# A decoder trunk on one core: the order of the first feed-forward block's first loads, products and transposes

## The chip, the core and the metric

The kernel runs on one core of a Trainium2 chip. The metric is the device time of one execution in microseconds (us); lower is better. A profiled execution also gives a trace: for every instruction its engine, its start and its duration, what its engine had been waiting for, and for every transfer its issue and its landing. The engines are named as in the trace: PE is TensorE (matmuls; PEld is its weight load), DVE is VectorE, ACT is ScalarE, POOL is GpSimd and SP is SyncE. An engine takes the instructions of its queue in order.

## What is computed

The reference is a trunk of two layers on 512 tokens of 1024 features, all in f32. Each layer runs a half-step gated feed-forward block, a token mixer, a cross-attention and another feed-forward block, with a layer norm after each:

```python
def swiglu_ffn(x, w_in, w_out):
    h = x @ w_in
    g, u = jnp.split(h, 2, axis=-1)
    return (jax.nn.silu(g) * u) @ w_out
...
for i in range(DEPTH):
    m, j = i % N_MIXERS, i // N_MIXERS
    x = layer_norm(a * x + 0.5 * swiglu_ffn(x, ffn_w_in[i, 0], ffn_w_out[i, 0]),
                   ln_g[i, 0], ln_b[i, 0])
    ...
    x = layer_norm(a * x + h, ln_g[i, 1], ln_b[i, 1])
    x = layer_norm(a * x + memory_cross_attention(x, mem, xa_wq[i], xa_wkv[i], xa_wo[i]),
                   ln_g[i, 2], ln_b[i, 2])
    x = layer_norm(a * x + 0.5 * swiglu_ffn(x, ffn_w_in[i, 1], ffn_w_out[i, 1]),
                   ln_g[i, 3], ln_b[i, 3])
return x
```

The change lies in the very first `swiglu_ffn`, in its first matrix product `x @ w_in` (1024 x 5632).

## The kernel before

**Numbers.** TensorE multiplies in a reduced format, so each f32 operand is split in two parts: ScalarE casts it (`hi`, line 120) and VectorE subtracts the cast from the original (`lo`, line 121). A product is three matmuls per block: high weights with high tokens, high weights with low tokens, low weights with high tokens (lines 205 to 207; the very first product has its own loop, line 681, with all 16 matmuls of the high weights first and then the 8 of the low ones).

**Tokens.** X0 to X3 are four tiles of 128 tokens x 1024 features. A tile comes to TensorE transposed: four transposes of 128x128 into a tile `pt` (line 489) for each half of the features, then a split of `pt` into `xh` and `xl`. `turn` does that for tiles 0 and 1.

**Products.** The block's two dimensions are halved (tokens 0 to 255 and 256 to 511, features 0 to 511 and 512 to 1023), and the product is built from seven block products instead of eight. The token side has seven "factors": 0 and 1 are the two feature halves of the first 256 tokens; 2 and 3 come from the last 256 tokens (3 from a difference that uses both halves); 4, 5 and 6 are further sums and differences. `second_factors` makes 2 to 6 in four steps: tile 2 (factors 3 and 2), tile 3 (the same), then s2, s4 and factor 6, then factors 4 and 5. It first makes two sums (line 611) on VectorE, each from a high and a low part.

**Units.** `up` is a generator that makes one unit, 256 columns of both the gate half and the up half. It goes through seven products: x (factor 0), y (1), z (3), then 6, 4, 5 and 2. The weight operands come from raw tiles: `ra` and `rc` are loaded plainly by SP (line 662), and POOL later adds another block of the matrix onto the same raw tile by an accumulating transfer (line 666), once the tile has been split. Raw tiles and split tiles (`wh`, `wl`) rotate in a few buffers: four `ra`, three `rc`, four each of `wh` and `wl`.

**Order.** `ffn` advances three such generators, called lanes (units one, two and three), by hand: each `next` issues the instructions up to the generator's next `yield`. A scheduler puts the instructions of each engine in a queue, mostly in program order; `issue_after(ins)` and `behind()` (after the last matmul) force that an instruction stands behind `ins` in the queue of the same engine, without a semaphore. In the first block (`at_start`) the loads are interleaved too: SP issues the identity, the first feature half of X0 and X1, `ra` of unit one, the second half of X0 and X1, `rc` of unit one, `ra` and `rc` of unit two, X2, X3, then `ra` and `rc` of unit three.

On TensorE that gives: first-half transposes, second-half transposes, x and y of unit one, x of unit two, transposes of tile 2, y of unit two, transposes of tile 3, x and y of unit three, z of the three units, factor-6 products of the three units, then their factor-4 products.

Of the kernel before, what the change touches and what calls it, by code (L numbers as in the profile page):

```python
# [9 lines left out]
F32 = mybir.dt.float32  # L10
# [7 lines left out]
P = 128  # L18
# [91 lines left out]
class Trunk:  # L110
# [402 lines left out]
    def ffn(self, layer, j, ln, beside=()):  # L513
        w_in, w_out = self.a["ffn_w_in"][layer, j], self.a["ffn_w_out"][layer, j]
        self.seven_of, self.factors = {}, self.factor_tiles()
        n, beside = len(FFN_TURNS), iter(beside)
        at_start = bool(self.load_rest)
        downs = {i: self.down(d, w_out, 2.0 * ALPHA if i == 1 else 1.0) for i, (_, d) in enumerate(FFN_TURNS) if d}

        def start(turn):  # L520
            ups = FFN_TURNS[turn][0]

            early = (2, 1, 1) if turn == 0 else (0, 0)
            rest = self.load_rest.pop if turn == 0 and at_start else lambda: lambda: None
            got = [self.up(w_in, u, lane, early[lane], rest() if lane == 0 else None) for lane, u in enumerate(ups)]
            for lane, g in enumerate(got):
                next(g)
                if lane == 1:
                    rest()()
            if turn > 1:  # L530
                next(downs[turn])
            return got + [downs[i] for i in downs if i == turn]

        works = start(0)
        if at_start:

            for tag, half in (("px", 0), ("py", 1)):
                for t in self.late[:2]:
                    self.turn(t, half, tag)
                next(works[0])  # L540
            next(works[1])
        else:
            for w in works + works[:1]:
                next(w)
            self.turn_late(2)
        self.late = []
        next(works[0])
        act, dve = self.first_split
        if self.begins:

            for late, first in zip(self.begins, (act, dve)):
                self.queue_behind(late, first)
        second = self.second_factors()
        if at_start:

            next(works[0])
            for w in (works[1], second, works[1], second, works[2], works[2]):
                with self.behind():
                    next(w)
        else:  # L560
            for w in (second, *works[1:], second, downs[1]):
                next(w)
        for turn in range(n):
            behind = turn == n - 1
            for step in range(1 if turn == 0 else 0, 9 if behind else 7):
                if turn == 0 and step in (2, 3):
                    next(second)
                if step == 4:
                    if behind:
                        coming = [self.plain_down(w_out, layer, j, ln, beside)]  # L570
                    else:
                        coming = start(turn + 1)
                        if at_start and turn == 0:
                            with self.tc.issue_after(self.last_load.ins):
                                next(downs[1])
                if behind and step in (4, 6, 7, 8):
                    next(coming[0])
                if behind and step > 3:
                    few(beside, 2)

                for lane, w in enumerate(works[: None if not behind or step > 1 else -1]):
                    if not (at_start and turn == 0 and lane < 2 and step == 1):
                        next(w, None)
                if turn == 1 and step == 3:
# [16 lines left out]
    def second_factors(self):  # L601

        nc, F, H = self.nc, self.factors, 2 * P
        s1, a21, a11, a12 = (self.tmp("hb", (P, 4, H)) for i in range(4))
        s2 = self.tmp("sr", (P, 4, H))

        def sums():
            for r, (hi, lo) in zip((a11, a12), F):  # L610
                nc.vector.tensor_tensor(r, hi.bitcast(F32), lo.bitcast(F32), ALU.add)

        if self.begins is None:
            with self.tc.issue_after(self.first_split[1].ins):
                sums()

        def part(i, x, o=slice(0, H)):
            self.split(F[i][0][:, :, o], F[i][1][:, :, o], x)

        for t in (2, 3):  # L620
            o = slice(t % 2 * P, (t % 2 + 1) * P)
            pts = []
            for half in range(2):
                pt = self.aux("pt", (("py", "yz"), ("px", "py"))[t % 2][half])
                pt = pt.rearrange("p (c n) -> p c n", c=4)
                c0 = half * S
# [3 lines left out]
            nc.scalar.copy(a21[:, :, o], pts[0])  # L630
# [12 lines left out]
        s3 = a21  # L643
        nc.vector.tensor_tensor(s3, a11, a21, ALU.subtract)
        part(5, s3)
        yield

    def up(self, w, u, lane, early, between):
# [5 lines left out]
        nc, H = self.nc, 2 * P  # L654
# [10 lines left out]
        def more(t, *block):  # L665
            nc.gpsimd.dma_start(t, source(*block), accum_op=ALU.add)  # L666

        def operand(raw):
            v = self.hl([P, 4, H])
            splits.append(self.split(v[0], v[1], raw))  # L670
            return v

        def product(ps, v, a, start=False):
            x = self.factors[a]
            if between and start and a == 0:

                for parts in (((0, 0), (0, 1)), ((1, 0),)):
                    for n in range(8):
                        j, k = divmod(n, 4)
                        for i, l in parts:  # L680
                            self.last_mm = nc.tensor.matmul(
                                ps[:, j], v[i][:, k, j * P : (j + 1) * P], x[l][:, k],
                                start=n == i == l == 0, stop=n == 7 and i == 1, skip_group_check=True,
                            )
                return
            for j in range(2):
                o = slice(j * P, (j + 1) * P)
                for k in range(4):

                    self.mm3(  # L690
                        ps[:, j], (v[0][:, k, o], v[1][:, k, o]), (x[0][:, k], x[1][:, k]),
                        start and j == k == 0, j == 1 and k == 3, True,
                    )

        bank = lambda t: t.rearrange("p (j n) -> p j n", j=2)
        splits = []

        third = lane == 2
        sp = lambda: self.tmp("ha" if third else "sp", (P, 2, H))
        yz = "py" if third else "yz"  # L700
        ra = load("ra", 1, 1)
        if between:
            between()
        rc = load("rc", 2, 1)
        yield
        v = operand(ra)
        if early and lane == 0:
            self.first_split = splits[0]
        more(ra, 1, 2)
        if early:  # L710
            yield
        v2 = early > 1 and operand(rc)
        if v2:
            yield
        x = bank(self.aux("x", "px") if third else self.mm("x"))
        product(x, v, 0, True)
        p1 = sp()
        nc.scalar.copy(p1, x)
        yield
        y = bank(self.aux("y", yz))  # L720
        product(y, v2 or operand(rc), 1, True)
# [788 lines left out]
    def run(self):  # L1510
        tc, nc, a = self.tc, self.nc, self.a
        with ExitStack() as ctx:
# [8 lines left out]
            c = lambda shape, name, dt=F32: self.constp.tile(shape, dt, name=name)  # L1521
            self.X = [self.tokp.tile([P, D], F32, name=f"X{t}") for t in range(NT)]
            def load_x(t, c=slice(0, D)):
                nc.sync.dma_start(self.X[t][:, c], a["x"][0, t * P : (t + 1) * P, c])
# [4 lines left out]
            load_half(0)  # L1529
# [114 lines left out]
```

## Time and profile before

| what | value |
|---|---|
| median of 3 runs | 1926.87 us (1926.81 to 1927.17) |
| the profiled execution's own time | 1925.08 us |
| its span in the trace | 1923.3 us |
| TensorE busy | 1892.8 us, 98% of the span |
| VectorE busy | 1563.6 us, 81% |
| ScalarE busy | 1023.1 us, 53% |
| share of the DMA engines in the first 40 us | 1.02, 256 GB/s |

The span is the time from the first to the last recorded instruction; the time of an execution is a little longer, and the median of the runs a little longer again. In a row of the timeline the columns are: start, duration, engine and line, operation, result and operands, count, and in brackets the idle time of the engine just before and what ended it. A row of the stretches shows, after the stretch and its length, the busy time and the instruction count of PE, PEld, DVE, ACT and POOL, then the granted clock, the share of the DMA engines and what they moved in GB/s. A row of the DMA issues ends with the time from issue to landing.

### The profile page before, as it was taken

What the parts mean: (1) busy time and instruction counts of PE and PEld (TensorE: products, weight loads), DVE (VectorE), ACT (ScalarE), POOL (GpSimd) and SP (SyncE); (2) the same over time, 40 slices, a digit from 0 to 9 for tenths busy, and PEclk for the clock granted to TensorE, in tenths of its full rate; (3) what the DMA queues carried; (4) which work ended last, traced back from release to release, by engine and by line L of the source; (5) the groups of instructions that cost most, each with busy time, mean ns of one, the idle gap of its engine ahead of it and who ended that gap; (6) DMA issues with size and microseconds to landing.
All of it is one profiled execution on the core that took longest, in us unless ns stands there. A gap on an engine that the chain in (4) does not pass through costs nothing.

```text
span 1923.3 us, 32450 instructions
## 1 busy us (share of the span) xinstructions
PE 1892.8 (98%) x13050; PEld 1737.6 (90%) x13050; DVE 1563.6 (81%) x2263; ACT 1023.1 (53%) x1580; POOL 319.7 (17%) x278
## 2 busy tenths in 40 slices
PE   8999999999999999999999999999999999999998
PEld 7999998888878888999998999999899889999997
DVE  6888989888967558889888988898787568898886
ACT  6555554567755435645554655455455436555553
POOL 2112121111210001221220311212130012111210
PEclk9999999999999999999999999999999999999999
DMA  9978772322124317977785587778334337877861
GB/s 237 221 169 187 166 148 77 91 66 88 61 94 154 110 66 193 181 179 162 144 194 175 108 179 166 179 163 184 111 132 132 132 88 160 173 170 168 185 133 55
DMA packets 246742, 277.94 MB, mean 145 GB/s; under 512 B 8256, under 2 KB 212544, under 8 KB 246592
## 3 DMA queue, kind: packets, MB, share of 16 engines
q0 software_dynamic: 92928, 92.29, 31.2%
q1 hardware_dynamic: 153664, 183.59, 29.3%
q8 instruction: 102, 1.67, 0.4%
q14 instruction: 48, 0.39, 0.1%
HBM read 273.75 MB, written 2.10 MB: 143 GB/s over the span
## 4 chain that ended last, share of the span: by engine, by line
PE 78%; DVE 13%; ACT 4%; DMA 2%; issue 2%; POOL 1%; SPq 0%; DVEq 0%; ACTq 0%; POOLq 0%
PE x L205 7%; PE x L206 7%; PE x L207 7%; PE z L207 4%; PE z L206 4%; PE z L205 4%; PE ps L205 4%; PE ps L207 4%; PE ps L206 4%; DVE wl L121 2%; PE px L205 2%; PE px L207 2%; PE px L206 2%; DMA ra<-in_ffn_w_in_dram 2%; PE y L207 2%
## 5 line engine op out<-in xcount | busy, mean ns | idle before, releaser
L666 POOL DMA_DIRECT2D ra<-in_ffn_w_in_dram x132 | 170.8, 1317 | 987.0 <-DVE wl L121 802.6
L120 ACT CAST wh<-ra 128x1024 fp32r<-128x1024 f32 x184 | 193.4, 1053 | 216.7 <-PE x L206 68.1
L121 DVE TENSOR_TENSOR wl<-ra,wh 128x1024 fp32r<-128x1024 f32 x184 | 223.7, 1221 | 72.8 <-ACT wh L120 72.2
L120 ACT CAST wh<-rc 128x1024 fp32r<-128x1024 f32 x136 | 143.0, 1053 | 116.9 <-PE x L206 41.6
L205 PE MATMUL x<-xe,wh 128*128 128x256 f32 x704 | 195.0, 277 | 0.0
L206 PE MATMUL x<-xe,wh 128*128 128x256 f32 x704 | 194.8, 277 | 0.0
L207 PE MATMUL x<-xe,wl 128*128 128x256 f32 x704 | 194.8, 277 | 0.0
L121 DVE TENSOR_TENSOR wl<-rc,wh 128x1024 fp32r<-128x1024 f32 x136 | 164.8, 1221 | 28.2 <-ACT wh L120 27.8
L120 ACT CAST wh<-b 128x1024 fp32r<-128x1024 f32 x112 | 117.8, 1052 | 128.3 <-PE x L206 65.6
L121 DVE TENSOR_TENSOR wl<-b,wh 128x1024 fp32r<-128x1024 f32 x112 | 136.9, 1222 | 39.4 <-ACT wh L120 39.1
L205 PE MATMUL x<-xh,wh 128*128 128x256 f32 x544 | 151.1, 278 | 0.0
L206 PE MATMUL x<-xl,wh 128*128 128x256 f32 x544 | 150.6, 277 | 0.0
L207 PE MATMUL x<-xh,wl 128*128 128x256 f32 x544 | 150.6, 277 | 0.0
L206 PEld LDWEIGHTS x<-xe,wh 128*128 128x128 f32 x704 | 132.5, 188 | 1.4
L205 PEld LDWEIGHTS x<-xe,wh 128*128 128x128 f32 x704 | 132.2, 188 | 1.3
L207 PEld LDWEIGHTS x<-xe,wl 128*128 128x128 f32 x704 | 132.2, 188 | 0.0
L121 DVE TENSOR_TENSOR wl<-raw,wh 128x1024 fp32r<-128x1024 f32 x64 | 82.8, 1298 | 42.9 <-ACT wh L120 42.2
L206 PEld LDWEIGHTS x<-xl,wh 128*128 128x128 f32 x544 | 102.5, 188 | 0.7
L205 PEld LDWEIGHTS x<-xh,wh 128*128 128x128 f32 x544 | 102.1, 188 | 0.7
L207 PEld LDWEIGHTS x<-xh,wl 128*128 128x128 f32 x544 | 102.2, 188 | 0.0
L207 PE MATMUL y<-xh,wl 128*128 128x256 f32 x352 | 98.5, 280 | 1.2 <-DVE wl L121 0.5
L205 PE MATMUL z<-xh,wh 128*128 128x256 f32 x352 | 97.6, 277 | 1.2 <-ACT xh L120 0.8
(429 smaller groups left out, 6265.7 us busy)
## 6 DMA issues: line engine op xcount, KB each, us to landing
ra<-in_ffn_w_in_dram POOLq DMA_DIRECT2D x132, 512.0 KB, 6.9
rc<-in_ffn_w_in_dram SPq DMA_DIRECT2D x88, 512.0 KB, 5.7
b<-in_ffn_w_out_dram SPq DMA_DIRECT2D x76, 512.0 KB, 4.7
ra<-in_ffn_w_in_dram SPq DMA_DIRECT2D x44, 512.0 KB, 5.0
rc<-in_ffn_w_in_dram POOLq DMA_DIRECT2D x44, 512.0 KB, 7.6
raw<-in_xa_wkv_dram SPq DMA_DIRECT2D x16, 1024.0 KB, 5.5
raw<-in_da_w_qkv_dram SPq DMA_DIRECT2D x16, 512.0 KB, 5.2
raw<-in_xa_wq_dram SPq DMA_DIRECT2D x8, 1024.0 KB, 5.2
```

The lines of the kernel that those rows point to most:

```text
L120: self.nc.scalar.copy(hi, src),
L121: self.nc.vector.tensor_sub(lo, src, hi.bitcast(F32)),
L205: mm(out, w[0], x[0], start=start, stop=False, skip_group_check=again)
L206: mm(out, w[0], x[1], start=False, stop=False, skip_group_check=again)
L207: self.last_mm = mm(out, w[1], x[0], start=False, stop=stop, skip_group_check=again)
L666: nc.gpsimd.dma_start(t, source(*block), accum_op=ALU.add)
```

## The change

It touches the first block alone, apart from one tile that is taken earlier in the code of the first lane.

- The second feature half of X0 is loaded only once the first half of X0 has landed: SP waits for that transfer before it issues this one, and everything behind it on SP follows.
- The first product of unit one is cut in two: its 16 matmuls with high weights go between the transposes of the first and the second feature half, its 8 with low weights stay behind the second half's.
- The split of unit one's `rc` is ordered behind the split of the last turned tokens, and the two sums on VectorE behind `rc`'s low part (before: behind `ra`'s).
- The transposes and factors of tiles 2 and 3 come before x and y of unit two instead of around its y; the splits of unit three's `ra` and `rc` are ordered behind the last of these factors.
- The y of unit three is ordered behind its x, and z of unit three moves from in front of the factor-6 products to between unit two's and its own.

On TensorE that gives: first-half transposes, 16 matmuls of x of unit one, second-half transposes, the other 8, y of unit one, transposes of tiles 2 and 3, x and y of unit two, x and y of unit three, z of units one and two, factor-6 products of units one and two, z of unit three, its factor-6 product, then the factor-4 products.

```diff
                 for t in self.late[:2]:
                     self.turn(t, half, tag)
                 next(works[0])
+                if half == 0:
+                    next(works[0])
             next(works[1])
...
             next(works[0])
-            for w in (works[1], second, works[1], second, works[2], works[2]):
+            for w in (second, second, works[1], works[1], works[2], works[2]):
                 with self.behind():
                     next(w)
...
-                    if not (at_start and turn == 0 and lane < 2 and step == 1):
-                        next(w, None)
+                    if at_start and turn == 0 and (lane < 2 and step == 1 or lane == 2 and step == 2):
+                        continue
+                    next(w, None)
+                    if at_start and turn == 0 and lane == 2 and step == 3:
+                        next(w)
...
         if self.begins is None:
-            with self.tc.issue_after(self.first_split[1].ins):
+            with self.tc.issue_after(self.low.ins):
                 sums()
 
         def part(i, x, o=slice(0, H)):
-            self.split(F[i][0][:, :, o], F[i][1][:, :, o], x)
+            self.made = self.split(F[i][0][:, :, o], F[i][1][:, :, o], x)
...
-        def operand(raw):
+        def operand(raw, behind=()):
             v = self.hl([P, 4, H])
+            if behind:
+                act, dve = behind
+                with self.tc.issue_after(act.ins):
+                    self.nc.scalar.copy(v[0], raw)
+                with self.tc.issue_after(dve.ins):
+                    self.low = self.nc.vector.tensor_sub(v[1], raw, v[0].bitcast(F32))
+                return v
             splits.append(self.split(v[0], v[1], raw))
             return v
...
+        def first_product(ps, v, parts):
+            x = self.factors[0]
+            for n in range(8):
+                j, k = divmod(n, 4)
+                for i, l in parts:
+                    self.last_mm = nc.tensor.matmul(
+                        ps[:, j], v[i][:, k, j * P : (j + 1) * P], x[l][:, k],
+                        start=n == i == l == 0, stop=n == 7 and i == 1, skip_group_check=True,
+                    )
+
...
+        at_start = early and self.begins is None
...
-        v = operand(ra)
+        v = operand(ra, self.made if third and at_start else ())
...
-        v2 = early > 1 and operand(rc)
+        x = bank(self.aux("x", "px") if third else self.mm("x"))
+        parted = between and at_start
+        if parted:
+            first_product(x, v, ((0, 0), (0, 1)))
+            yield
+        v2 = early > 1 and operand(rc, self.turned if parted else ())
         if v2:
             yield
-        x = bank(self.aux("x", "px") if third else self.mm("x"))
-        product(x, v, 0, True)
+        if between:
+            if not parted:
+                first_product(x, v, ((0, 0), (0, 1)))
+            first_product(x, v, ((1, 0),))
+        else:
+            product(x, v, 0, True)
...
-        product(y, v2 or operand(rc), 1, True)
+        v2 = v2 or operand(rc, self.made if third and at_start else ())
+        with self.behind() if third and at_start else nullcontext():
+            product(y, v2, 1, True)
...
-            self.load_rest = [lambda: (load_x(2), load_x(3)), lambda: load_half(1)]
+            first = load_half(0)
+
+            def second_half():
+                info = mybir.DependencyInfo(mybir.DependencyClass.Sync, mybir.DependencyReason.DATA)
+                self.tc.add_manual_dep(load_half(1)[0].ins, first[0].ins.name, info, reason="second_half")
+
+            self.load_rest = [lambda: (load_x(2), load_x(3)), second_half]
```

More of the change, by code (lines that the diff above doesn't have):

```diff
@@ L674, in product @@
             x = self.factors[a]
[L675 to L685, printed above, removed]
             for j in range(2):
@@ L1523, in load_x @@
             def load_x(t, c=slice(0, D)):
-                nc.sync.dma_start(self.X[t][:, c], a["x"][0, t * P : (t + 1) * P, c])
+                return nc.sync.dma_start(self.X[t][:, c], a["x"][0, t * P : (t + 1) * P, c])
             self.ident = c([P, P], "ident")
@@ L1528, in run @@
             load_half = lambda half: [load_x(t, slice(half * S, (half + 1) * S)) for t in range(2)]
-            load_half(0)
-            self.load_rest = [lambda: (load_x(2), load_x(3)), lambda: load_half(1)]
+            first = load_half(0)
[3 more added lines that the diff above has]
+            self.load_rest = [lambda: (load_x(2), load_x(3)), second_half]
             self.mhalf = c([P, NT], "mhalf")
```

## The prediction

> **What bounds the kernel now.** I read the page first, then the busy time by stretches, then the timeline of the head engine by engine with the landings of its transfers.
>
> ```profile
> span 1923.3 us, 32450 instructions
> PE 1892.8 (98%) x13050; PEld 1737.6 (90%) x13050; DVE 1563.6 (81%) x2263; ACT 1023.1 (53%) x1580; POOL 319.7 (17%) x278
> ```
>
> ```profile
> 0.00:40.00 40.00, 31.16 (x241) 29.99 (x242) 25.29 (x28) 23.87 (x32) 8.16 (x11) 1.00 1.02 256
> 40.00:48.00 8.00, 7.71 (x68) 7.51 (x67) 8.00 (x8) 6.59 (x8) 4.33 (x4) 1.00 0.95 140
> 48.00:280.00 232.00, 231.70 (x1754) 219.78 (x1753) 200.57 (x252) 125.54 (x153) 44.64 (x35) 1.00 0.84 182
> ```
>
> TensorE (first busy figure of a row) is the bound: 30.5 us idle in the whole span, 8.84 of it in the first 40 us, 0.29 in the next 8, and then 0.3 in 232 us. So whatever the head gains or loses by 48 us is handed on one for one, and the head cannot return more than about 9 us however it is rearranged. The change's work all lies in these first 48 us.
>
> Inside the head TensorE's timeline shows where its time goes:
>
> ```profile
> 4.22 2.29 PE L489 MATMUL pt<-ident,X 128*128 128x128 f32 x8 [4.22 <-DMA X<-in_x_dram]
> 9.55 1.97 PE L489 MATMUL pt<-ident,X 128*128 128x128 f32 x8 [3.05 <-DMA X<-in_x_dram]
> ...
> 11.53 0.41 PE L681 MATMUL x<-xl,wh 128*128 128x256 f32 x1
> ...
> 13.24 0.41 PE L681 MATMUL x<-xl,wh 128*128 128x256 f32 x1
> ...
> 13.60 0.28 PE L681 MATMUL x<-xl,wh 128*128 128x256 f32 x1
> ...
> 14.19 1.07 PE L681 MATMUL x<-xh,wl 128*128 128x256 f32 x8
> ...
> 15.32 0.28 PE L207 MATMUL y<-xh,wl 128*128 128x256 f32 x1
> ```
>
> The first half's transposes run at 4.22, the second half's at 9.55, then the first product: 16 matmuls with the high weights, 8 with the low ones, and at 15.32 the third matmul of the second product, the first to read its low weights. From 11.53 to 13.24 are eight matmuls, 0.214 us apart and 0.41 long; from 13.60 they are 0.28 long. Up to about 13.5 TensorE runs at half pace.
>
> ```profile
> 20.54 1.04 PE L489 MATMUL pt<-ident,X 128*128 128x128 f32 x8
> ...
> 30.56 0.28 PE L207 MATMUL y<-xh,wl 128*128 128x256 f32 x1
> 31.62 0.38 PE L205 MATMUL z<-xh,wh 128*128 128x256 f32 x1 [0.78 <-ACT xh L120]
> 32.71 0.39 PE L206 MATMUL z<-xl,wh 128*128 128x256 f32 x1 [0.70 <-DVE xl L121]
> 32.93 0.28 PE L207 MATMUL z<-xh,wl 128*128 128x256 f32 x1
> ...
> 40.88 0.28 PE L205 MATMUL z<-xe,wh 128*128 128x256 f32 x1
> 41.45 0.38 PE L206 MATMUL z<-xe,wh 128*128 128x256 f32 x1 [0.29 <-DVE xe L121]
> ...
> 49.60 0.28 PE L205 MATMUL x<-xe,wh 128*128 128x256 f32 x1
> ```
>
> Two more holes. The third product of the first unit (z, from 31.62) waits for the last tokens' factors: its third matmul stands at 32.93 where, three warm intervals of 0.115 after 30.56, it would stand at 30.90; 2.0 us are lost. The first use of factor 6 loses about 0.55 (41.45 instead of 0.115 after 40.88, and a slower restart). 49.60 is the first matmul of product 4, by which I measure the head.
>
> **The change part by part.** *The gate on the token loads.* SP's queue and the landings:
>
> ```profile
> 2.11 0.43 SPq L662 DMA_DIRECT2D ra<-in_ffn_w_in_dram  x1
> 2.59 0.98 SPq L1524 DMA_DIRECT2D X<-in_x_dram  x2
> ```
>
> ```profile
> ra<-in_ffn_w_in_dram SPq DMA_DIRECT2D x1, 512.0 KB, 6.7
> X<-in_x_dram SPq DMA_DIRECT2D x1, 256.0 KB, 6.9
> X<-in_x_dram SPq DMA_DIRECT2D x1, 256.0 KB, 7.1
> ```
>
> The first weights ra land at 2.11 + 6.7 = 8.8, the second-half tokens at 2.59 + 6.9 = 9.5 and 0.7 later at 10.2. The gate holds SP until the first tokens are there (4.2, from the 4.22 row), 1.6 us longer; behind it on SP wait the second half, rc and ra of units one and two, X2, X3, and unit three's loads. What ra gains isn't in the trace. Nothing: it stays at 8.8. At most: 256 KB land 0.7 apart, so after the tokens of 4.2 come the other tile (0.7) and ra (1.4), 6.3; but ScalarE is still casting tokens until 7.1. So the cast can start between 7.1 and 8.8; I take 8.0, the middle, for no row is nearer to either end. The gate's own cost is nothing as long as the delayed tokens land by the end of the first 16 matmuls (10.2 + 1.6 = 11.8 at worst, wanted at 12.5 below); without that cover it would be the difference, up to 0.2 in the fastest case.
>
> The rows of the table above land in the order in which they were issued. [...]
>
> *First product between the halves.* ScalarE and VectorE:
>
> ```profile
> 8.82 1.04 ACT L120 CAST wh<-ra 128x1024 fp32r<-128x1024 f32 x1 [1.69 <-DMA ra<-in_ffn_w_in_dram]
> ...
> 11.56 0.59 ACT L120 CAST xh<-pt 128x512 fp32r<-128x512 f32 x1 [0.27 <-PE pt L489]
> 12.04 1.05 ACT L120 CAST wh<-rc 128x1024 fp32r<-128x1024 f32 x1
> ```
>
> ```profile
> 13.92 1.22 DVE L121 TENSOR_TENSOR wl<-rc,wh 128x1024 fp32r<-128x1024 f32 x1
> 15.05 1.22 DVE L121 TENSOR_TENSOR wl<-ra,wh 128x1024 fp32r<-128x1024 f32 x1
> ```
>
> The 16 matmuls need the first-half factors and the cast of ra: 8.0 + 1.05 + 0.05 = 9.1 (8.2 to 9.9). That is hardly before 9.55, when the transposes start today: TensorE begins as early as now, only with its two pieces swapped. At half pace they take 16 x 0.214 = 3.4, to 12.5 (11.6 to 13.3). The second half's transposes follow: 1.97 us at half pace, 1.04 at full pace, and if full pace comes at 13.5 as now, about 1.5: end at 14.0 (13.5 to 14.4) instead of 9.55 + 1.97 = 11.52.
>
> The half pace ends 3.9 us after TensorE's second start (9.55 to about 13.5). [...]
>
> What hangs on the transposes is the second product. Its weights rc are cast behind the last token cast, by explicit order now and in fact already today: from the transposes' end at 11.52, cast of the tokens at 11.56, cast of rc 12.04 to 13.09, then the subtraction, 1.22, which today waits behind a sum on VectorE until 13.92 and tomorrow doesn't. So low weights stand 1.57 + 0.05 + 1.22 = 2.8 after the transposes' end, and the third matmul 2.9 after: 16.9 (16.4 to 17.3) instead of 15.32. Between them TensorE has only the 8 low-weight matmuls (0.9) and two more: a new hole of about 1.8 us opens at the head of y. This is the price of the swap, and nothing in the order covers it; queued behind y on TensorE is everything else.
>
> *Last tokens' factors ahead of the second unit.* It moves 16 transposes (2 x 0.8 as they displace products at full pace; work moved, not added) from around the second unit's y to before its x, and with them 2 copies, 4 casts, 6 subtractions.
>
> ```profile
> 22.75 1.23 DVE L121 TENSOR_TENSOR wl<-ra,wh 128x1024 fp32r<-128x1024 f32 x1 [3.61 <-ACT wh L120]
> ...
> 30.84 1.22 DVE L121 TENSOR_TENSOR wl<-ra,wh 128x1024 fp32r<-128x1024 f32 x1
> ...
> 32.57 0.68 DVE L121 TENSOR_TENSOR xl<-pt,xh 128x512 fp32r<-128x512 f32 x1
> ...
> 35.03 1.23 DVE L121 TENSOR_TENSOR wl<-ra,wh 128x1024 fp32r<-128x1024 f32 x1 [0.64 <-ACT wh L120]
> ...
> 40.17 1.22 DVE L121 TENSOR_TENSOR xe<-hb,xe 128x1024 fp32r<-128x1024 f32 x1
> ```
>
> Today the last of these factors is made at 32.57, behind a weight subtraction at 30.84. Now the transposes end near 21.2 and the ten small steps are queued early; VectorE's 3.61 us of idleness ahead of 22.75 takes them. The 2.0 us at z go. Late next is unit three's ra, now ordered behind these factors: VectorE does from 16.9 four wide steps (1.13 apart, from 13.92 and 15.05: two weights, two sums), seven narrow ones (0.6: the first unit's sum and six for the factors) and then ra's subtraction, done at 16.9 + 4.5 + 4.2 + 1.2 = 26.8; TensorE wants it at 16.9 + 2.5 + 1.6 + 5.5 = 26.5 (rest of y, transposes, x and y of unit two). I put 0.3 for this, bounds 0 and 1.7 (rival three). Factor 6 has after it eight wide and two narrow steps, 37.1; TensorE reaches it two products after unit three's, at 37.5, so the 0.55 at 41.45 goes too (bound: it stays).
>
> *Third unit's z later.*
>
> ```profile
> 33.95 1.05 ACT L120 CAST wh<-ra 128x1024 fp32r<-128x1024 f32 x1 [1.41 <-DMA ra<-in_ffn_w_in_dram]
> ```
>
> ```profile
> 24.27 1.28 POOL L666 DMA_DIRECT2D ra<-in_ffn_w_in_dram  x1 [6.40 <-DVE wl L121]
> ```
>
> Its weights are an accumulating transfer that POOL issued at 24.27, after the subtraction of 22.75, and that ScalarE had at 33.95, 9.7 later. Issued after 26.8 they come at 36.7 and are split by 39. Z moves behind two factor-6 products, wanted near 43: cost nothing, and 1.5 to 2 us if it had stayed.
>
> *Elsewhere* only a product tile is taken earlier in the first lane's code; no row moves, 0.
>
> **The sum.** Today 15.32 to 49.60 is 34.28. Less 2.0 and 0.55, plus 0.3: 32.0. Product 4 then starts at 16.9 + 32.0 = 48.9 against 49.6: 0.6 to 0.7 earlier, say 0.6. The profiled execution took 1925.08 with a span of 1923.3; the median of the runs is 1926.87. The shift carries over: 1926.3.
>
> **Rivals.** *One, the gate brings nothing:* ra at 8.8, the low weights of the second product read at 17.3, 0.4 later than in the sum: -0.3 (from 49.3), 1926.6. For it: landings in order of issue; against: ra took 6.7 for 512 KB when 256 KB pass in 0.7.
> *Two, both early:* cast at 7.1, so 16 matmuls to 11.6, full pace already at 12, transposes to 13.0, low weights read at 15.9, no wait at unit three: 15.9 + 34.28 - 2.55 = 47.6, 2.0 earlier, 1924.9. For it: ra's slow landing; against: TensorE idles from 6.5 (4.22 + 2.29), so the half pace should last.
> *Three, slower:* unit three's ra gets stuck behind the factors.
>
> ```profile
> 23.10 0.59 ACT L630 COPY hb<-pt 128x512 f32<-128x512 f32 x1
> ```
>
> If the copy that opens the factors (now at 23.10, after the first unit's activation) still stands behind that activation on ScalarE, the factors start only after VectorE's fifth step (16.9 + 4.5 + 0.6 = 22.0), all ten steps end near 27, ra's subtraction at 28.2, and unit three's x waits 1.7, not 0.3: +0.8, 1927.7; with one more wide step ahead +1.9. It decides from a wait of 0.9 upwards. For it: ScalarE and VectorE are strictly in order and VectorE is nearly full; against: the activation waits on y alone, done by 19.5.
>
> **How the numbers follow.** Forecast 0.45 (between -1.2 and -0.4), rival one 0.15, two 0.15, three 0.17, other orders 0.08. The range from 1924.6 to 1928.1 holds two's lower and three's upper mechanism. A difference of 0.2%, 3.85 us, is about what a measurement of this kernel tells from no change; the holes that the change can close (2.0 + 0.55, and at most 1.5 at the start) barely reach it with nothing lost, and the new hole takes most. Faster by more 0.04, within 0.92, slower by more 0.04.
>
> **What would show it.** First product starting near 9.1 (8.2 if the gate works fully, 9.9 if not); transposes of the second half right behind it, ending near 14; a hole of 1 to 2 us before y's third matmul at about 16.9; no hole before z; a short wait for unit three's ra near 26.5; product 4 near 49. The prediction is wrong if y shows no hole, if z still waits, or if product 4 starts after 50.

## The result: slower by 0.2 to 0.5%

Beside the kernel before on the same chip the changed kernel took 1936.15 us (median of 6 runs, 1932.03 to 1937.38) against 1926.97: ratio 1.0047, 95% interval 1.0036 to 1.0059. On another chip the ratio was 1.0024 (1.0015 to 1.0034). The forecast of 1926.3 us, no measurable difference, was wrong.

The profiled execution took 1937.38 us, the longest of its six; that of the kernel before, 1925.08, lies 1.8 below its median. So the two traces stand further apart (12.3 us) than the medians (9.2, and about 5 on the other chip), and sizes read from them hold for these two executions. Of the page and of the busy time by stretches, the rows that answer to those shown of before (after the stretch and its length the busy times of PE, PEld, DVE, ACT and POOL, then granted clock, DMA share, GB/s):

```profile
span 1935.6 us, 32453 instructions
PE 1901.7 (98%) x13050; PEld 1746.4 (90%) x13050; DVE 1564.3 (81%) x2263; ACT 1024.2 (53%) x1580; POOL 320.2 (17%) x278
```

```profile
0.00:40.00 40.00, 30.84 (x221) 29.35 (x222) 27.33 (x30) 25.29 (x33) 6.91 (x10) 0.96 0.95 245
40.00:48.00 8.00, 8.00 (x73) 8.00 (x73) 6.20 (x6) 3.64 (x4) 6.50 (x5) 1.00 1.08 163
48.00:280.00 232.00, 228.66 (x1692) 217.09 (x1691) 193.15 (x242) 122.06 (x149) 41.57 (x33) 0.99 0.83 178
```

The span grew by 12.3 us, TensorE's busy time by 8.9 with the same 13050 instructions: most of the loss is not waiting, it is matmuls that ran slower. In two of the three stretches the granted clock is below 1, and the stretch from 48 us, which had 0.3 us of idleness before, now has 3.3. TensorE's timeline says where:

```profile
4.20 2.10 PE L489 MATMUL pt<-ident,X 128*128 128x128 f32 x8 [4.20 <-DMA X<-in_x_dram]
8.12 0.58 PE L701 MATMUL x<-xh,wh 128*128 128x256 f32 x1 [1.81 <-ACT wh L120]
...
11.66 1.04 PE L489 MATMUL pt<-ident,X 128*128 128x128 f32 x8
...
14.37 0.38 PE L205 MATMUL y<-xh,wh 128*128 128x256 f32 x1 [0.73 <-ACT wh L678]
...
15.63 0.39 PE L207 MATMUL y<-xh,wl 128*128 128x256 f32 x1 [0.76 <-DVE wl L680]
...
25.54 0.28 PE L207 MATMUL y<-xh,wl 128*128 128x256 f32 x1
26.48 0.39 PE L205 MATMUL x<-xh,wh 128*128 128x256 f32 x1 [0.66 <-ACT wh L678]
...
27.99 0.39 PE L207 MATMUL x<-xh,wl 128*128 128x256 f32 x1 [1.01 <-DVE wl L680]
...
28.68 0.41 PE L206 MATMUL x<-xl,wh 128*128 128x256 f32 x1
...
34.94 0.28 PE L205 MATMUL z<-xh,wh 128*128 128x256 f32 x1
...
48.54 0.28 PE L205 MATMUL x<-xe,wh 128*128 128x256 f32 x1
...
49.90 0.28 PE L205 MATMUL x<-xe,wh 128*128 128x256 f32 x1
53.37 0.58 PE L205 MATMUL z<-xe,wh 128*128 128x256 f32 x1 [3.20 <-ACT ha L755]
53.75 0.41 PE L206 MATMUL z<-xe,wh 128*128 128x256 f32 x1
...
58.44 0.41 PE L207 MATMUL z<-xe,wl 128*128 128x256 f32 x1
```

The first product starts at 8.12, the hole at y is there, z (34.94) waits no more. But unit three's x waits twice, at 26.48 and 27.99, and unit three's factor-6 product waits 3.20 us at 53.37. Behind both waits a matmul is 0.41 long instead of 0.28, the length of the first microseconds:

```profile
28.00:32.00 4.00, 4.00 (x21) 4.00 (x22) 4.00 (x5) 1.80 (x3) 1.28 (x1) 0.58 0.53 86
...
52.00:56.00 4.00, 2.63 (x12) 2.63 (x13) 1.23 (x1) 1.32 (x2) 1.28 (x1) 0.57 1.23 194
56.00:60.00 4.00, 4.00 (x23) 4.00 (x23) 0.24 (x1) 1.05 (x1) 0.00 (x0) 0.58 1.24 197
```

The two stretches in which TensorE was busy throughout hold 21 and 23 instructions, where those from 36, 40 and 44 us, at a granted clock of 1.00, hold 38, 37 and 38. By the clock records half pace holds from 28.67 to 32.09 and from 52.57 to 59.39.

ScalarE's timeline and the chain of waits (start, duration, what) explain 53.37:

```profile
45.95 1.05 ACT L120 CAST wh<-ra 128x1024 fp32r<-128x1024 f32 x1 [1.66 <-PE z L206]
51.79 1.04 ACT L120 CAST wh<-ra 128x1024 fp32r<-128x1024 f32 x1 [4.79 <-DMA ra<-in_ffn_w_in_dram]
52.74 0.58 ACT L755 COPY ha<-z 128x512 f32<-128x512 f32 x1
```

```profile
42.28 0.90 POOL rc L671
43.18 8.51 DMA ra<-in_ffn_w_in_dram
51.88 0.86 issue
52.74 0.59 ACT ha L755
53.37 0.58 PE z L205
```

Unit three's z is done well before 49.90, which is already the 13th matmul of product 4 (the first is at 48.54): in the trace these 13 stand ahead of unit three's factor-6 product, not behind it as in the order told above. The z has to be copied out before the factor-6 product accumulates onto the same tile, and that copy takes 0.58 us. It stands on ScalarE behind the cast of unit three's product-4 weights, and that cast waits until 51.7 for a transfer that was issued at 43.18. TensorE thus waits for weights that the stopped product does not use.

With the matmuls of the two traces paired by number (the n-th of one with the n-th of the other; times of the changed kernel), the changed kernel stands at -1.6 us at 12, +0.4 at 17 (the hole at y), +4.3 at 32 (unit three's x and half pace), +2.2 at 38 (the old hole at z is gone), +1.65 at 44, +8.0 at 61, +10.4 at 151, +12.3 at the end.

### The profile page after: what moved, and what is told of

Read it like the earlier page. It is cut to its first block, busy times and chain, and to the rows that moved or that the text cites. A ratio compares the mean times of both kernels' runs of the same rounds, so it can differ in the third digit from the quotient of the medians.

```text
span 1935.6 us, 32453 instructions
## 1 busy us (share of the span) xinstructions
PE 1901.7 (98%) x13050; PEld 1746.4 (90%) x13050; DVE 1564.3 (81%) x2263; ACT 1024.2 (53%) x1580; POOL 320.2 (17%) x278
## 3 DMA queue, kind: packets, MB, share of 16 engines
q8 instruction: 102, 1.67, 0.4%
## 4 chain that ended last, share of the span: by engine, by line
PE 77%; DVE 14%; ACT 4%; issue 2%; DMA 2%; POOL 1%; SPq 0%; DVEq 0%; ACTq 0%; POOLq 0%
PE x L206 7%; PE x L205 7%; PE x L207 7%; PE z L205 4%; PE z L207 4%; PE z L206 4%; PE ps L205 3%; PE ps L207 3%; PE ps L206 3%; DVE wl L121 3%; PE px L205 2%; PE px L207 2%; PE px L206 2%; PE x L701 2%; PE y L207 2%
## 5 line engine op out<-in xcount | busy, mean ns | idle before, releaser
L205 PE MATMUL z<-xe,wh 128*128 128x256 f32 x352 | 99.0, 281 | 3.2 <-ACT ha L755 3.2
```

The costliest lines, as they stand in the source:

```text
L205: mm(out, w[0], x[0], start=start, stop=False, skip_group_check=again)
```

## The experiments

Theory: the 3.2 us come from the copy behind the cast, and every hole costs a second time by half pace. Rivals: the transfer itself sets the time; the early hole at unit three's x makes the loss; the time goes elsewhere. Each kernel was compared with the kernel before on its own chip, 5 to 11 runs. A hole is idle time of TensorE, in us, read from one profile of each kernel; z without a unit is unit one's.

| kernel | ratio (95% interval) | hole at unit three's x, or at z | hole at its factor 6 | later half pace, up to 70 us |
|---|---|---|---|---|
| changed | 1.0047 (1.0036 to 1.0059) | 0.66 + 1.01 | 3.20 | 3.41 + 6.83 us |
| changed, again | 1.0024 (1.0015 to 1.0034) | 0.66 + 1.00 | 4.6 | 6.83 |
| no_made | 1.0037 (1.0025 to 1.0050) | 0.80 (z), 0.56 + 0.84 (factor 6 of unit one) | 4.46 | 6.83 |
| fill | 1.0032 (1.0020 to 1.0045) | 0.66 + 1.01 | filled | 3.41 |
| z_in_place | 1.0004 (0.9995 to 1.0013) | 0.66 + 1.01 | none | 3.41 |
| copy_first | 1.0006 (0.9997 to 1.0015) | 0.86 + 1.01 | none | 3.41 |
| copy_nosplit | 0.9997 (0.9988 to 1.0007) | 0.64 + 1.00 | none | none |
| best1 | 0.9992 (0.9983 to 1.0000) | none | none | none |
| best1, again | 0.9987 (0.9979 to 0.9996) | 0.88 (z), 0.56 (factor 6 of unit one) | none | none |
| best2 | 1.0001 (0.9992 to 1.0010) | 0.56 (z) | 1.95, at its z | none |
| gate_only | 0.9998 (0.9989 to 1.0007) | 0.88 + 0.70 (z) | none | 3.41 |
| factors_only | 0.9999 (0.9990 to 1.0007) | 0.36 (x of unit three) | 1.09, at its z | none |
| z_late_only | 1.0008 (0.9999 to 1.0016) | 0.31 + 0.70 (z), 0.89 + 0.89 (factor 6 of unit one) | 1.07 | none |

**The late hole, removed in two ways.** z_in_place puts unit three's z back ahead of the factor-6 products:

```diff
-                    if at_start and turn == 0 and (lane < 2 and step == 1 or lane == 2 and step == 2):
-                        continue
-                    next(w, None)
-                    if at_start and turn == 0 and lane == 2 and step == 3:
-                        next(w)
+                    if not (at_start and turn == 0 and lane < 2 and step == 1):
+                        next(w, None)
```

> The changed kernel with unit three's z back in front of the factor-6 products. Theory (ScalarE's order): unit three's factor-6 product waited for the copy of its z (53.33), which stood on ScalarE behind the cast of weights for unit three's product 4 (landed 51.7). With z early its copy stands before that cast: the hole of 3.2 us ahead of the factor-6 product and the half pace from 52.6 to 59.4 (3.4 us lost) go; 6 us or more faster than the changed kernel, 1928 to 1930. Rival (the transfer itself is late, whatever the order): the wait comes back at unit three's product 4 and 2 us at most are won, 1934 or more.

copy_first leaves z late and only puts the cast behind the copy:

```diff
-        nc.scalar.copy(p5, z)
+        z_copy = nc.scalar.copy(p5, z)
...
-        product(x, operand(ra), 4)
+        with self.tc.issue_after(z_copy.ins) if third and at_start else nullcontext():
+            w4 = operand(ra)
+        product(x, w4, 4)
```

> The changed kernel; the cast of unit three's product-4 weights is ordered behind the copy of unit three's z on ScalarE, z stays late. Theory (ScalarE's order): the hole of 3.2 us and the half pace behind it go as in the run with z in place, 1928 to 1930. Rival (it is z's late place that costs, through its own weights or its buffer): no more than 1 us won, 1935 or more. Rival (the transfer is late): the wait moves to product 4 of unit three, 1932 to 1934.

Both lose the hole, the 6.83 us of half pace and nearly all of the slowdown. ScalarE's timeline of copy_first:

```profile
49.68 0.59 ACT L755 COPY ha<-z 128x512 f32<-128x512 f32 x1 [1.85 <-PE z L207]
52.59 1.05 ACT L120 CAST wh<-ra 128x1024 fp32r<-128x1024 f32 x1 [2.33 <-DMA ra<-in_ffn_w_in_dram]
```

The same transfer lands as late as before (52.5) and TensorE waits for it nowhere: product 4 of units one and two covers it. The order of two instructions on ScalarE was the fault, not the transfer.

**The early hole alone.** no_made is the changed kernel without the order that puts unit three's splits behind the factors:

```diff
-        v = operand(ra, self.made if third and at_start else ())
+        v = operand(ra)
...
-        v2 = v2 or operand(rc, self.made if third and at_start else ())
+        v2 = v2 or operand(rc)
```

> The changed kernel without the order of unit three's two splits behind the last tokens' factors. Theory: the hole of 2.1 us ahead of unit three's x (26.5 to 28.0) goes, and with it the half pace from 28.7 to 32.1 (1.7 us lost); product z starts 3 to 4 us earlier; but the factor-6 product of unit three still waits for the same cast, whose transfer is issued at a time that other steps set, so the later hole grows: 1933 to 1936. Rival (the late hole is a chain that starts in the early one): all of it is won at the end, 1930 to 1933, or more.

Unit three's x no longer waits, and nothing of it is left in the time. TensorE's and ScalarE's timeline:

```profile
39.24 0.39 PE L205 MATMUL z<-xe,wh 128*128 128x256 f32 x1 [0.56 <-ACT sp L755]
40.58 0.39 PE L207 MATMUL z<-xe,wl 128*128 128x256 f32 x1 [0.84 <-DVE wl L121]
```

```profile
53.16 1.04 ACT L120 CAST wh<-ra 128x1024 fp32r<-128x1024 f32 x1 [6.05 <-DMA ra<-in_ffn_w_in_dram]
54.11 0.58 ACT L755 COPY ha<-z 128x512 f32<-128x512 f32 x1
```

By pairs of matmuls no_made is 1.9 us ahead of the changed kernel's profile at its 36 us (+0.35 against +2.21) and level with it at 42 (+2.3 against +2.2): the two waits above, at unit one's factor-6 product, took what had been won. Then the late hole comes as before, and longer, since its transfer was issued at 44.47 instead of 43.18: as long as the copy stands behind the cast, the landing sets the time. So this run doesn't show what the early hole costs by itself.

**Idleness can cost twice.** fill keeps the changed kernel's order and puts 46 transposes of the identity into an unused tile ahead of unit three's factor-6 product:

```diff
+        if third and at_start:
+            junk = self.aux("junk", "py")
+            with self.behind():
+                for _ in range(46):
+                    nc.tensor.transpose(junk[:, :P], self.ident, self.ident)
         product(z, operand(rd), 6)
```

> The changed kernel with 46 transposes of the identity into an unused tile between unit three's z and its factor-6 product: work for nobody, about 4.6 us of it, where TensorE now stands idle for 3.2 us after 1.5 us of product 4 (which then comes later). The factor-6 product starts at the same 53.4, since its copy is as late. Theory (idleness costs twice, once by itself and once by the half pace from 52.6 to 59.4): the product runs at full pace, 0.28 us a matmul and 2.7 us in all instead of 5.1, 3.4 us are won and 1.5 lost by the product-4 matmuls that are displaced; 1.5 to 2.5 us faster than the changed kernel. Rival (the half pace has nothing to do with the hole): 0.41 us a matmul as before, 1.5 us slower than the changed kernel.

TensorE's timeline and its stretches:

```profile
53.25 0.93 PE L761 MATMUL junk<-ident 128*128 128x128 f32 x7
53.93 0.37 PE L205 MATMUL z<-xe,wh 128*128 128x256 f32 x1
54.14 0.29 PE L206 MATMUL z<-xe,wh 128*128 128x256 f32 x1
```

```profile
52.00:56.00 4.00, 4.00 (x38) 4.00 (x37) 1.23 (x1) 1.53 (x2) 1.14 (x1) 1.00 1.23 194
```

The product starts no earlier (53.93 against 53.37), but from its first matmul to the next product's pass 2.8 us instead of 5.3. So 2.5 us of what the late wait costs are half pace, and they go when TensorE is given work for nobody in the wait. The ratio, 1.0032, lies between the two measured for the changed kernel, so the gain is shown by the trace and not by the times.

**One part alone.** gate_only is the kernel before with the last hunk of the change:

```diff
-            load_half(0)
-            self.load_rest = [lambda: (load_x(2), load_x(3)), lambda: load_half(1)]
+            first = load_half(0)
...
+            self.load_rest = [lambda: (load_x(2), load_x(3)), second_half]
```

> The kernel before with nothing but the gate: SP holds the second-half token loads until the first half of X0 has landed; every engine's queue is as before. Theory (the gate alone is a gain, the loss comes from the reordering): ra is cast near 7.0 instead of 8.8 and the second-half tokens are in by 8.7 instead of 10.2, so the second-half transposes run from about 7.7 instead of 9.55, the first product starts near 9.5 instead of 11.17; 1 to 2 us earlier at product 4, 1925.0 to 1926.0 in all. Rival (the gate only helped because the first product was moved): transposes start as before at 9.5, 1926.5 to 1927.3. Rival (the early start is lost to the wait for the last tokens' factors): first product early, but the hole before z grows from 2.0 to 3.5 or more, 1926.5 to 1927.3.

ScalarE's and TensorE's timeline:

```profile
6.97 1.05 ACT L120 CAST wh<-ra 128x1024 fp32r<-128x1024 f32 x1
```

```profile
10.25 1.12 PE L489 MATMUL pt<-ident,X 128*128 128x128 f32 x4 [1.51 <-DMA X<-in_x_dram]
...
32.25 0.38 PE L205 MATMUL z<-xh,wh 128*128 128x256 f32 x1 [0.88 <-ACT xh L120]
33.34 0.39 PE L206 MATMUL z<-xl,wh 128*128 128x256 f32 x1 [0.70 <-DVE xl L121]
```

The gate does what it says: ra's cast stands at 6.97 instead of 8.82. But 8.82 is one execution; factors_only, whose loads are those of the kernel before, has in its ScalarE timeline

```profile
7.55 1.04 ACT L120 CAST wh<-ra 128x1024 fp32r<-128x1024 f32 x1 [0.59 <-DMA ra<-in_ffn_w_in_dram]
```

and z_late_only 8.02. Alone the gate brings nothing that the times show. The trace offers two reasons: the last of the second-half tokens are transposed only at 10.25 (expected by 8.7), and the hole at z, 1.58 us in place of 1.48, is followed by half pace from 34.78 to 38.20.

factors_only moves only the last tokens' factors ahead of unit two:

```diff
-            for w in (works[1], second, works[1], second, works[2], works[2]):
+            for w in (second, second, works[1], works[1], works[2], works[2]):
```

> The kernel before with one part of the change alone: the two factor steps of the last tokens are issued ahead of unit two's steps. Theory (this part does what it is for, the hole of 2.0 us at z goes, and what the change adds elsewhere loses it): no hole at unit one's z, the time 1 to 2 us below the kernel before, ratio 0.9990 to 0.9995. Rival (the wait only moves: unit two's or unit three's first product now waits for its split behind the factors' work on ScalarE and VectorE, as unit three's did in the changed kernel with 1.67 us, with half pace behind it when both idle pieces lie in one stretch of 3.41 us): a hole of 1 to 2 us in x of unit two or three, ratio 0.9997 to 1.0015.

The rival holds, though not where it had put the hole (x of unit two or three): the hole at unit one's z goes, and in TensorE's timeline a new one stands at unit three's z, with smaller ones around it (0.36 us at 24.88, 0.31 at 40.69):

```profile
37.29 0.39 PE L207 MATMUL z<-xh,wl 128*128 128x256 f32 x1 [1.09 <-DVE wl L121]
```

z_late_only moves only unit three's z (the diff of z_in_place, read the other way):

> The kernel before with one part of the change alone: unit three's third product z is issued behind the factor-6 products of units one and two. ScalarE's order then has three casts of product-4 weights ahead of the copy of unit three's z, as the changed kernel has, and one of them is unit three's own. Theory (the late z alone makes the loss: its copy waits in ScalarE's row behind a cast that waits for a transfer, and TensorE falls to half pace after the hole): unit three's factor-6 product begins 2 to 5 us after the matmul ahead of it, matmuls of 0.41 us follow for 3.4 or 6.8 us, and the time is 4 to 9 us above the kernel before, ratio 1.002 to 1.005. Rival (the late z costs only together with the other parts, which bring TensorE there earlier or make the transfer later): the hole is under 1 us, no half pace follows, and the ratio is within 0.001 of 1.

The theory that the late z loses it all alone falls. TensorE's timeline and the chain of waits:

```profile
38.47 0.39 PE L205 MATMUL z<-xe,wh 128*128 128x256 f32 x1 [0.89 <-ACT sp L735]
...
39.97 0.38 PE L206 MATMUL z<-xe,wh 128*128 128x256 f32 x1 [0.89 <-DVE xe L121]
...
50.96 0.40 PE L205 MATMUL z<-xe,wh 128*128 128x256 f32 x1 [1.07 <-ACT ha L735]
```

```profile
42.73 6.56 DMA ra<-in_ffn_w_in_dram
...
50.33 0.59 ACT ha L735
```

The copy is stuck behind the same cast, but the transfer is issued 0.45 us earlier and takes 6.56 us instead of 8.51, so the hole is 1.07 us and half pace stays away. POOL had issued the two transfers onto the raw tiles of the factor-6 weights, which go ahead of it, at 37.95; in the changed kernel they go out at 40.01 and 42.27, directly ahead of it, and those tiles are split later too (VectorE subtracts at 38.25 and 40.52 instead of from 36.43 on). That the traffic ahead makes the 2 us is read from the two traces and was not tried by itself. New are two holes of 0.89 us: unit three's z used to cover the copy of unit one's z and the making of factor 6.

**The cut product, and versions.** copy_nosplit is copy_first with unit one's first product whole again, behind both halves' transposes:

```diff
-                if half == 0:
-                    next(works[0])
...
-        parted = between and at_start
+        parted = False
...
```

> The run copy_first with the first product whole again behind both halves' transposes. Theory (the split costs a hole at y that its earlier start doesn't pay back): no hole at y, since the cast and subtraction of rc now run beside 16 matmuls; with ra at 7.0 and the second tokens by 8.7 to 10.2 TensorE begins at 7.7 to 9.5 instead of 8.1 and y's third matmul comes at 14 to 15.5 instead of 15.9; 0.5 to 1.5 us faster than copy_first if the hole at unit three's x stays the same. Rival (the split pays, because the tokens' second half lands late): y's third matmul at 16 or later, 0 to 1 us slower. Rival (a later wait sets the time: VectorE has factor 6 no earlier than before): the gain is gone by product 4, no difference.

Its y starts at 13.28 and waits for nothing, against 14.37 and 15.63 in the changed kernel. The wait at unit three's x is there (0.64 + 1.00 us), yet no half pace follows. So the ratio's 0.9997 against 1.0006 (the intervals overlap) holds both the hole at y and a half pace that fell away by its place in time, and doesn't price the cut alone. Nor does y's place in one profile: in best1, with the product whole too, y's third matmul came at 16.09 (here 13.50, in copy_first 15.94), where half of the second-half tokens were transposed only at 9.93 and full pace came only at 15.7.

best1 is copy_nosplit with no_made's edit, and the last factor step issued behind unit one's factor-6 operand:

```diff
-                if turn == 0 and step in (2, 3):
+                if turn == 0 and step == (2 if at_start else step) and step in (2, 3):
                     next(second)
...
+                    if at_start and turn == 0 and lane == 0 and step == 3:
+                        next(second)
```

> copy_nosplit, and unit three's splits not ordered behind the last factors, and the last step of the factors (4 and 5) issued behind unit one's factor-6 operand. Theory: no hole at y (2 us), none at unit three's x (2.1 and 1.7 of half pace), factor 6 used from about 38 instead of 41; but z late leaves unit three's product-4 weights to land near 53, when TensorE wants them near 51 or 52; product 4 starts at 47 to 48: 1924.5 to 1926. Rival (VectorE is the bound up to 41): holes of together 2 to 3 us appear before the factor-6 products, 1926.5 to 1928.

best2 is best1 with z back in place instead of the reordered copy.

> best1 with unit three's z in front of the factor-6 products again instead of the forced order of the copy. Theory: as best1, and unit three's product-4 weights are issued earlier, so nothing waits there; 1924 to 1925.5. Rival (z's weights, an accumulating transfer, land at 35 to 37 and hold ScalarE and VectorE as in the kernel before): a hole before unit three's z of 1 to 2 us, equal to best1 or slower, 1926 to 1928.

best2's rival came true: unit three's z waits 1.95 us for its low weights at 38.25. best1 was run again, with the changed kernel beside it:

> The version with the gate, the first product whole behind both halves' transposes, the factors ahead of unit two with the last step behind unit one's factor-6 operand, unit three's splits without the added order, and unit three's copy of z ahead of the cast of its product-4 weights, a second time on another chip or at another hour. Theory (the parts bring 1 to 2 us once the two holes are gone): ratio 0.9985 to 0.9999, as the 0.9992 before. Rival (the gain was the spread of one day's runs): ratio 1.0000 or above.

> The changed kernel as it is, a second time, for its ratio beside the other three on one chip. Theory: 1.0036 to 1.0059 as before, the late hole of 3 us and half pace of 6.8 us behind it in the profile. Where the matmuls between 60 and 150 us take 0.118 us each in this profile too, that belongs to this kernel; where they take 0.113, it belonged to that one execution, and the time of the kernel is then lower by about 2.4 us in this profile than in the first one.

best1 has the lowest ratio of all, 0.9992 and 0.9987: 1.5 to 2.5 us below the kernel before (the first interval reaches 1.0000, and both overlap that of copy_nosplit), with TensorE idle 0.3 us in the 232 after 48, as before. Its rows by stretch (second profile):

```profile
0.00:40.00 40.00, 32.81 (x248) 31.92 (x248) 28.30 (x31) 25.88 (x35) 8.16 (x11) 1.00 1.01 254
40.00:48.00 8.00, 8.00 (x69) 7.70 (x69) 5.41 (x5) 3.62 (x5) 6.50 (x5) 1.00 1.16 180
48.00:280.00 232.00, 231.71 (x1752) 219.80 (x1751) 201.00 (x252) 126.99 (x154) 42.48 (x33) 1.00 0.84 181
```

7.2 us idle in the first 40 instead of 8.84, none in the next 8 instead of 0.29.

## Why the prediction was wrong

**What held.** TensorE is the bound (busy for 98% of the span), and the lag of the head (+8.0 us at 61) wasn't won back later. The gate works, and fully: the first product began at 8.12, the early bound (8.2), not at 9.1. Its size is less sure than one pair of profiles makes it: ra was cast at 6.85 to 7.19 in the eleven profiles with the gate and at 7.55, 8.02 and 8.82 in the three without, so the 8.82 on which the prediction built was the latest of three. Rival one rested on the landings in order of issue (8.8, 9.5 and 10.2 in the kernel before) and left ra at 8.8. With the loads issued behind it held back ra was cast sooner (the times just given), so the measurement decides against that rival; by which mechanism the later loads cost ra time no run shows. The hole at y came, with the third matmul at 15.63 instead of 16.9: the cast was a microsecond early and full pace came at 11.6 instead of 13.5. The latter was luck: in the fourteen profiles full pace first came between 11.6 and 15.7, in the changed kernel's second one at 14.1, and there that matmul stood at 16.32. The 2.0 us at z and the 0.55 at factor 6 went. (One reading of rows was off without consequence: from 11.53 to 13.24 stand nine matmuls, not eight.)

**A mark met by luck.** The prediction measured the head by the first matmul of product 4. It came at 48.54, forecast 48.9, before 49.60, and yet the kernel lost: unit three's factor-6 product, which had stood ahead of this matmul, now stood behind it. With its 24 matmuls ahead (24 x 0.113 = 2.7 us, an estimate) product 4 would have begun near 51.3, past the 50 that the prediction named as a sign of being wrong. The lag of +1.65 at 44 us says the same.

**The step that failed: "Third unit's z later ... cost nothing".** I followed the z's own weights, which came in time, and not what z issues behind itself: a copy to ScalarE, which the factor-6 product waits for. I never listed what had come to stand ahead of that copy in ScalarE's queue, namely a cast that waits for a transfer issued at 43.18. It cost 3.2 us of wait and 2.5 of half pace; z_in_place and copy_first take both away. The other half of the step, 1.5 to 2 us if z had stayed in its place, failed too: in z_in_place nothing waits there (in best2 z waits 1.95). Rival three looked for a stuck instruction too, but at unit three's ra on VectorE.

**A term mis-sized: unit three's x, 0.3 us.** The place was right (26.5 forecast, 26.48 seen), the size was rival three's, and half of its mechanism. ScalarE's and VectorE's timeline:

```profile
19.50 1.28 ACT L748 ACT_TABLE_LOAD   x1
20.79 0.63 ACT L748 ACTIVATE hr<-hr 128x512 f32<-128x512 f32 x1
21.33 0.57 ACT L635 COPY hb<-pt 128x512 f32<-128x512 f32 x1
```

```profile
22.45 0.69 DVE L121 TENSOR_TENSOR xl<-hb,xh 128x512 fp32r<-128x512 f32 x1 [1.11 <-ACT xh L120]
...
26.72 1.21 DVE L680 TENSOR_TENSOR wl<-ra,wh 128x1024 fp32r<-128x1024 f32 x1
```

The copy that opens the second tile's factors stands behind the first unit's activation and its table load, VectorE idles 1.11 us for it, and the subtraction for unit three ends at 27.93 (rival three: 28.2) instead of 26.8. The third matmul of x comes at 27.99 where, three times 0.115 after 25.54, it would stand at 25.89: 2.1 us, above the bound of 1.7, and half pace to 32.09 adds 1.5 (by pairs of matmuls the lag grows from +2.83 to +4.36 in it).

**A step that was missing: holes counted once.** The sum let TensorE keep full pace once it had it. It fell back twice, at 28.67 and at 52.57. Without the fall at 28.67 the changed kernel would have stood at about zero at 44 us instead of +1.65 (an estimate: 1.65 less 1.5). The early terms, that is, were fair in sum; the loss is that fall and, from 44 to 61 us, the late wait with the second one (+6.3).

**What is left open.** From +8.0 at 61 us the lag grows to +10.4 at 151, where a matmul came every 0.118 us instead of 0.113. In the changed kernel's second profile that lasted only to 90 us, and other kernels show such stretches elsewhere (best2 from 81 to 146): it changes with the execution. What sets it wasn't found, and it may be why the two ratios of the changed kernel, 1.0047 and 1.0024, lie apart; that isn't shown. The expectations for the second run were only half met: its ratio, 1.0024, lies below the 1.0036 to 1.0059 expected, and in its profile the pitch did go back, but a wait of 2.33 us near 387 us, which is 1.37 in the kernel before, with half pace behind it, lost about as much again. Of the change's parts, the cut of the first product and the new order of the splits were not tried alone.

## What to carry to other kernels

When a product is moved, list for each engine what then stands ahead of every instruction that it issues, copies of the result included: here one cast that waited 4.79 us for a transfer held up the copy behind it, for which TensorE, the bound engine, then idled 3.20 us. Give such a copy its place by order, or keep the waiting cast behind it. And price a hole of the matmul engine with what the clock takes afterwards: here two waits of 0.66 and 1.01 us cost 2.1 us, and the half pace behind them another 1.5. And parts of a change that measure as nothing alone (0.9998, 0.9999, 1.0008 for the three tried here) can cost 0.2 to 0.5% together.

## What the runs showed of the hardware

The fall to half pace needs no long idleness; the least that it followed is 1.58 us. In the clock records of the fourteen profiles every change of the clock stands a whole number of 3.413 us after the first change to full pace (in the changed kernel that one comes at 11.61, and those at 28.67, 32.09, 52.57 and 59.39 stand 5, 6, 12 and 14 times 3.413 us behind it). Before the end of the execution half pace lasts 3.41 us, or twice that where TensorE idled on into the next stretch (in the changed kernel 28.67 to 32.09, and 52.57 to 59.39 with the first 0.80 us of it idle). Cut at that grid, up to 70 us, all stretches that begin at full pace and hold at most 1.48 us of idleness are followed by full pace (the largest: 1.48 at z in the kernel before, then 1.42, 1.42 and 1.33), and all with 1.58 or more (1.58 in gate_only, 1.67 three times, 1.87, 2.36, 2.39, 3.41) by half pace. The 1.48 us of the kernel before thus lie 0.1 us below the least that half pace followed. Past 70 us it is the same: the one fall before the end (the changed kernel's second profile, at 389.61) follows 2.26 us of idleness, and no other stretch holds more than 1.37. And the same two pieces, 0.66 + 1.01, cost half pace when they share a stretch (changed kernel, 1.67) and nothing when the grid divides them (second profile: 0.70 and 0.95; copy_nosplit: 1.26 and 0.39). In gate_only a stretch that was busy for more than half of its length was enough (1.58 us idle of 3.41).
